# Contrast adjustment of 48 image planes: twelve 4 MB tiles in six buffers become six 8 MB tiles in three

## The chip, the cores and the metric

The kernel runs on one core of one Trainium2 chip. The metric is device time in microseconds (us) of one execution; the time of the kernel before is the median of three runs. The engines named below are TensorE (PE, matrix multiply), VectorE (DVE), ScalarE (ACT), GpSimd (POOL) and SyncE (SP). SP issues the loads and ACT issues the stores; both kinds of transfer run on the core's 16 DMA engines, loads through the queue that the profile calls q1 and stores through q10. On-chip memory has 128 partitions.

## The reference

The input is 16 images of 3 colour planes of 512 x 512 float32, so 48 planes of 262,144 pixels, 50.33 MB. Each plane is stretched around its own mean and clipped to 0..1:

```python
mean = np.mean(x, axis=(2, 3), keepdims=True)
return np.clip(mean + factor * (x - mean), 0, 1)     # factor = 1.5
```

That is `factor * x + (1 - factor) * mean`, so a plane must have been read in full before its first pixel can be written. Input and output together are 100.66 MB of traffic.

## The kernel before, in words

The input is seen as one flat array. `ROW = 8192` consecutive pixels (32 KB) lie in one partition, so a tile of 128 partitions holds 4 MB, which is four whole planes of 32 partitions each. There are twelve tiles and a `ring` of six buffers; tile `t` lives in buffer `t % 6` and is worked on in place. For each tile:

- `load` (L74, issued by SP) brings it in. At the start the kernel issues tile 0, tile 1, tiles 2 and 3 as one transfer and tiles 4 and 5 as one.
- `add` (L89, ACT) goes over the tile with a copy that also sums each partition's row.
- `shift_by` (L94, PE) multiplies the column of 128 row sums with `blockw`, a 128 x 128 matrix that holds `(1 - factor) / pixels` in blocks of 32 x 32 on its diagonal and zero elsewhere. So each partition gets the bias of its plane, in `bias` in PSUM. `blockw` is filled by POOL at the start (L59 and L61).
- `clip` is two VectorE instructions over the tile: times factor plus bias (L78), then max with 0 and min with 1 (L82).
- `store` (L99, issued by ACT) writes it out.

Tile 0 is treated apart: VectorE sums its first 4352 columns (L108) while ACT sums the other 3840, and it is clipped and stored in three column pieces of 1024, 2048 and 5120 pixels (`CUTS`). The other tiles go through in one piece.

The order is written out by hand (`manual_schedule`): each engine runs its instructions in program order, and waits are put in where data or a buffer is needed. In ACT's program, `add(t + 1)` comes before `store(t)`, so a store is issued after the next tile has landed. In SP's program, the load of tile `t + 6` waits until the store of tile `t`, which used the same buffer, has landed.

Of the kernel before, what the change touches and what calls it, by code (L numbers as in the profile page):

```python
# [1 line left out]

# [4 lines left out]


P = 128  # L10
ROW = 8192
BUFS = 6
CUTS = (0, 1024, 3072, ROW)
SUM = 4352


@with_exitstack
def kernel(
    ctx: ExitStack,
    tc: tile.TileContext,  # L20
    x: bass.AP,
    factor: float,
    out: bass.AP,
):

    nc = tc.nc
    f32 = mybir.dt.float32
    Alu = mybir.AluOpType  # L30
    Act = mybir.ActivationFunctionType

    B, C, H, W = x.shape
    n_img, n_pix = B * C, H * W
    ppi = n_pix // ROW
    per_tile = P // ppi
    n_tiles = n_img // per_tile
    assert ppi * ROW == n_pix and per_tile * n_tiles == n_img

    factor = float(factor)  # L40
    wconst = (1.0 - factor) / float(n_pix)

    x_f = x.rearrange("b c h w -> (b c h w)")
    out_f = out.rearrange("b c h w -> (b c h w)")

    def dram(ap, t, c0=0, c1=ROW):
        return bass.AP(tensor=ap.tensor, offset=t * P * ROW + c0, ap=[[ROW, P], [1, c1 - c0]])

    consts = ctx.enter_context(tc.tile_pool(name="consts", bufs=1))
    xpool = ctx.enter_context(tc.tile_pool(name="xpool", bufs=1))  # L50
    small = ctx.enter_context(tc.tile_pool(name="small", bufs=1))
    psum = ctx.enter_context(tc.tile_pool(name="psum", bufs=1, space=bass.MemoryType.PSUM))


    sums = small.tile([P, 2 * n_tiles], f32, name="sums")
    bias = psum.tile([P, n_tiles], f32, name="bias")

    blockw = consts.tile([P, P], f32, name="blockw")
    nc.gpsimd.memset(blockw, 0.0)  # L59
    for a in range(0, P, ppi):  # L60
        nc.gpsimd.memset(blockw[a : a + ppi, a : a + ppi], wconst)  # L61


    ring = xpool.tile([P, BUFS, ROW], f32, name="ring")

    def load(t, c0=0, c1=ROW, n=1):

        b = t % BUFS
        src = bass.AP(
            tensor=x_f.tensor,  # L70
            offset=t * P * ROW + c0,
            ap=[[ROW, P], [P * ROW, n], [1, c1 - c0]],
        )
        nc.sync.dma_start(out=ring[:, b : b + n, c0:c1], in_=src)  # L74

    def clip(t, c0, c1):
        part = ring[:, t % BUFS, c0:c1]
        nc.vector.tensor_scalar(  # L78
            out=part, in0=part, scalar1=factor, scalar2=bias[:, t : t + 1],
            op0=Alu.mult, op1=Alu.add,  # L80
        )
        nc.vector.tensor_scalar(  # L82
            out=part, in0=part, scalar1=0.0, scalar2=1.0, op0=Alu.max, op1=Alu.min
        )

    def add(t, c0=0):
        part = ring[:, t % BUFS, c0:ROW]
        own = sums[:, 2 * t : 2 * t + 1]
        nc.scalar.activation(out=part, in_=part, func=Act.Copy, accum_out=own)  # L89
        return own  # L90

    def shift_by(t, *parts):
        for k, part in enumerate(parts):
            nc.tensor.matmul(  # L94
                bias[:, t : t + 1], blockw, part, start=k == 0, stop=k == len(parts) - 1
            )

    def store(t, c0, c1):
        nc.scalar.dma_start(out=dram(out_f, t, c0, c1), in_=ring[:, t % BUFS, c0:c1])  # L99

    with tc.manual_schedule():
        load(0)
        load(1)
        load(2, n=2)
        load(4, n=2)

        rest = sums[:, 1:2]
        nc.vector.tensor_reduce(  # L108
            out=rest, in_=ring[:, 0, 0:SUM], axis=mybir.AxisListType.X, op=Alu.add
        )  # L110
        shift_by(0, add(0, SUM), rest)
        for c0, c1 in zip(CUTS[:-2], CUTS[1:-1]):
            clip(0, c0, c1)
            store(0, c0, c1)
        clip(0, CUTS[-2], ROW)
        own = add(1)
        store(0, CUTS[-2], ROW)
        load(BUFS)
        for t in range(1, n_tiles):
            shift_by(t, own)  # L120
            clip(t, 0, ROW)
            if t + 1 < n_tiles:
                own = add(t + 1)
            store(t, 0, ROW)
            if t + BUFS < n_tiles:
                load(t + BUFS)


# [1 line left out]
_INS = ['x', 'factor']  # L130
_OUTS = [((16, 3, 512, 512), 'float32')]

_NUMBERS = {'factor': 1.5}


# [26 lines left out]
```

## Time and profile before

| what | value |
|---|---|
| time, median of 3 runs | 239.19 us (239.05 to 239.28) |
| the profiled execution: its span, first to last instruction | 237.8 us |
| VectorE busy | 112.1 us (47%) |
| ScalarE busy | 82.9 us (35%) |
| TensorE busy | 7.6 us (3%) |
| traffic | 100.66 MB, mean 423 GB/s over the span |
| ACTIVATE over 128 x 8192 | 7.03 us |
| TENSOR_SCALAR over 128 x 8192, first and second | 4.49 and 4.43 us |
| store of 4096 KB, issue to landing (median) | 44.2 us |
| load of 4096 KB, issue to landing (median) | 33.3 us |

The span is the profiled execution's own time, counted on the core; what lies around it is not recorded for that execution. A row of the profile that is a group of instructions names the source line, the engine and the operation, what is written and read, the shapes and the count, then busy time and the mean of one in ns, then the idle time of the engine before them and what ended it. A row in the order of time starts with the start and the duration in us; what stands in brackets is how long the engine had been idle and who released it. "ACTq" and "SPq" are the sequencers of ACT and SP, which issue transfers. A row of a stretch gives the stretch, its length, the busy time of PE, of the weight loads, of DVE, ACT and POOL with instruction counts, then the TensorE clock, the mean busy share of the DMA engines, and GB/s. In the row that starts with DMA, each digit is the busy share of one fortieth of the span, in tenths.

The trace also holds a record of each DMA packet, with its queue, size, start and duration.

### The profile page before, as it was taken

Reading aid. Unit: us, or ns where it says so; the run is one execution under the profiler, and the core shown is the slowest. Engines: PE = TensorE matmul, PEld = TensorE weight load, DVE = VectorE, ACT = ScalarE, POOL = GpSimd, SP = SyncE. Lnnn points to the kernel's source line nnn. Section 1 sums busy time; section 2 is a strip of 40 time slices with the busy share of each in tenths; the row PEclk is TensorE's granted clock in tenths of the full one; section 3 lists DMA queues with packets and bytes.
Section 4 is the critical chain, followed back from the end, with each engine's and each line's share of the span. In section 5 each row is a group of like instructions: output and inputs, shape, how many; then the busy total and the mean of one; then the engine's idle time right before and its main releaser. Section 6 shows DMA issues by size and latency. Waiting matters only on the chain.

```text
span 237.8 us, 219 instructions
## 1 busy us (share of the span) xinstructions
PE 7.6 (3%) x26; PEld 6.5 (3%) x26; DVE 112.1 (47%) x29; ACT 82.9 (35%) x25; POOL 0.9 (0%) x9
## 2 busy tenths in 40 slices
PE   0010000000000000000000000000000000000000
PEld 0000000000000000000000000000000000000000
DVE  0078786009990039979407705902920950770000
ACT  2051900399000697380091083056038009100000
POOL 1000000000000000000000000000000000000000
DMA  7999999999999999999999999999999999999996
GB/s 265 441 441 442 401 471 429 391 413 430 457 441 435 413 408 430 435 435 441 441 441 441 441 435 435 402 419 430 435 441 441 441 441 441 441 430 413 413 430 259
DMA packets 3712, 100.66 MB, mean 423 GB/s; under 512 B 384, under 2 KB 384, under 8 KB 512
## 3 DMA queue, kind: packets, MB, share of 16 engines
q1 hardware_dynamic: 1696, 50.33, 49.6%
q10 hardware_dynamic: 2016, 50.33, 49.1%
HBM read 50.33 MB, written 50.33 MB: 423 GB/s over the span
## 4 chain that ended last, share of the span: by engine, by line
DMA 52%; another core or an unknown queue 15%; DVE 11%; issue 9%; PE 1%; ACT 1%; SPq 0%; ACTq 0%
DMA ring<-in_x_dram 33%; DMA out_dram<-ring 20%; DVE ring L78 6%; DVE ring L82 6%; PE bias L94 1%; ACT ring L89 1%; SPq L74 0%; ACTq L99 0%; ACTq L89 0%
## 5 line engine op out<-in xcount | busy, mean ns | idle before, releaser
L89 ACT ACTIVATE ring<-ring 128x8192 f32<-128x8192 f32 (+1 forms) x12 | 80.7, 6725 | 119.4 <-DMA ring<-in_x_dram 119.4
L78 DVE TENSOR_SCALAR ring<-ring,bias 128x8192 f32<-128x8192 f32 (+3 forms) x14 | 54.3, 3880 | 87.1 <-PE bias L94 87.1
L82 DVE TENSOR_SCALAR ring<-ring 128x8192 f32<-128x8192 f32 (+3 forms) x14 | 53.4, 3817 | 0.5
L94 PE MATMUL bias<-sums,blockw 128*128 128x1 f32 x26 | 7.6, 361 | 196.1 <-ACT ring L89 195.6
L94 PEld LDWEIGHTS bias<-sums,blockw 128*128 128x128 f32 x26 | 6.5, 311 | 197.1 <-ACT ring L89 179.9
L108 DVE TENSOR_REDUCE sums<-ring 128x1 f32<-128x4352 f32 x1 | 4.7, 4686 | 13.0 <-DMA ring<-in_x_dram 13.0
L89 ACT ACTIVATION_READ_ACCUMULATOR ring<-ring 128x1 f32 x12 | 2.2, 186 | 0.0
L89 ACT ACT_TABLE_LOAD x1 | 1.3, 1283 | 0.7 <-PEq L143 0.7
L61 POOL MEMSET blockw<- 32x32 f32 x4 | 0.5, 116 | 0.2
L59 POOL MEMSET blockw<- 128x128 f32 x1 | 0.2, 205 | 0.3 <-POOLq L143 0.3
L143 POOL MEMSET const-bfloat16-1.0<- 128x1 bf16 x1 | 0.1, 111 | 0.0
L143 POOL MEMSET const-uint8-127<- 128x1 uint8 x1 | 0.1, 111 | 0.0
L143 POOL MEMSET const-float32-1.0<- 128x1 f32 x1 | 0.1, 108 | 0.0
L143 POOL MEMSET const-float32-0.0<- 128x1 f32 x1 | 0.1, 103 | 0.2 <-issue 0.2
## 6 DMA issues: line engine op xcount, KB each, us to landing
out_dram<-ring ACTq DMA_DIRECT2D x11, 4096.0 KB, 44.2
ring<-in_x_dram SPq DMA_DIRECT2D x8, 4096.0 KB, 33.3
ring<-in_x_dram SPq DMA_DIRECT2D x2, 8192.0 KB, 60.6
out_dram<-ring ACTq DMA_DIRECT2D x1, 2560.0 KB, 37.5
out_dram<-ring ACTq DMA_DIRECT2D x1, 1024.0 KB, 25.9
out_dram<-ring ACTq DMA_DIRECT2D x1, 512.0 KB, 16.1
```

Of the source, the lines that this page charges most:

```text
L59: nc.gpsimd.memset(blockw, 0.0)
L61: nc.gpsimd.memset(blockw[a : a + ppi, a : a + ppi], wconst)
L78: nc.vector.tensor_scalar(out=part, in0=part, scalar1=factor, scalar2=bias[:, t : t + 1], op0=Alu.mult, op1=Alu.add,)
L82: nc.vector.tensor_scalar(out=part, in0=part, scalar1=0.0, scalar2=1.0, op0=Alu.max, op1=Alu.min)
L89: nc.scalar.activation(out=part, in_=part, func=Act.Copy, accum_out=own)
L94: nc.tensor.matmul(bias[:, t : t + 1], blockw, part, start=k == 0, stop=k == len(parts) - 1)
L108: nc.vector.tensor_reduce(out=rest, in_=ring[:, 0, 0:SUM], axis=mybir.AxisListType.X, op=Alu.add)
L143: nc = _bacc.Bacc("TRN2", target_bir_lowering=False, num_devices=1)
```

## The change

A row becomes 16384 pixels (64 KB), so a tile holds 8 MB, which is eight planes of 16 partitions each, and there are six tiles. The ring has three buffers of 64 KB per partition, as many bytes as before. Tile 0 is loaded in two column halves (a half is 32 KB per partition), and so is the last tile; the other loads are one transfer of the whole tile. ACT sums every tile in two halves, whose two sums are added by the matmul; the last tile's second half is shared between VectorE (4352 columns) and ACT (3840). The last tile is clipped and stored in two halves; every other tile is clipped in two instructions over 16384 columns and stored as a whole. `blockw` is filled with the constant, and two `affine_select` instructions zero what lies off the diagonal blocks, in place of four small memsets. In ACT's program, a store goes ahead of the next tile's first `add`, except for tiles 0, 1 and 4, where it comes after it.

```diff
-ROW = 8192
-BUFS = 6
-CUTS = (0, 1024, 3072, ROW)
+ROW = 16384
+HALF = ROW // 2
+BUFS = 3
 SUM = 4352
...
-    nc.gpsimd.memset(blockw, 0.0)
-    for a in range(0, P, ppi):
-        nc.gpsimd.memset(blockw[a : a + ppi, a : a + ppi], wconst)
+    nc.gpsimd.memset(blockw, wconst)
+    for base, sign in ((0, 1), (ppi - 1, -1)):
+        nc.gpsimd.affine_select(
+            out=blockw, in_=blockw, compare_op=Alu.is_ge, fill=0.0, base=base,
+            pattern=[[-sign * ppi, per_tile], [0, ppi]], channel_multiplier=sign,
+        )
...
+    def add(t, k, c0, c1):
+        part = ring[:, t % BUFS, c0:c1]
+        own = sums[:, 3 * t + k : 3 * t + k + 1]
+        nc.scalar.activation(out=part, in_=part, func=Act.Copy, accum_out=own)
+        return own
...
-        load(0)
-        load(1)
-        load(2, n=2)
-        load(4, n=2)
-
-        rest = sums[:, 1:2]
+    last = n_tiles - 1
+    with tc.manual_schedule():
+        load(0, 0, HALF)
+        load(0, HALF, ROW)
+        for t in range(1, BUFS):
+            load(t)
+        shift_by(0, add(0, 0, 0, HALF), add(0, 1, HALF, ROW))
+        clip(0)
+        for t in range(last):
+            late = t + 1 < BUFS or t + 1 == last
+            if not late:
+                store(t)
+            first = add(t + 1, 0, 0, HALF)
+            if late:
+                store(t)
+            if t + BUFS < last:
+                load(t + BUFS)
+            elif t + BUFS == last:
+                load(last, 0, HALF)
+                load(last, HALF, ROW)
+            if t + 1 < last:
+                shift_by(t + 1, first, add(t + 1, 1, HALF, ROW))
+                clip(t + 1)
+        rest = sums[:, 3 * last + 2 : 3 * last + 3]
         nc.vector.tensor_reduce(
-            out=rest, in_=ring[:, 0, 0:SUM], axis=mybir.AxisListType.X, op=Alu.add
+            out=rest, in_=ring[:, last % BUFS, HALF : HALF + SUM],
+            axis=mybir.AxisListType.X, op=Alu.add,
         )
-        shift_by(0, add(0, SUM), rest)
-        for c0, c1 in zip(CUTS[:-2], CUTS[1:-1]):
-            clip(0, c0, c1)
-            store(0, c0, c1)
-        clip(0, CUTS[-2], ROW)
-        own = add(1)
-        store(0, CUTS[-2], ROW)
-        load(BUFS)
-        for t in range(1, n_tiles):
-            shift_by(t, own)
-            clip(t, 0, ROW)
-            if t + 1 < n_tiles:
-                own = add(t + 1)
-            store(t, 0, ROW)
-            if t + BUFS < n_tiles:
-                load(t + BUFS)
+        shift_by(last, first, add(last, 1, HALF + SUM, ROW), rest)
+        for c0 in (0, HALF):
+            clip(last, c0, c0 + HALF)
+            store(last, c0, c0 + HALF)
```

More of the change, by code (lines that the diff above doesn't have):

```diff
@@ L37 @@
     n_tiles = n_img // per_tile
-    assert ppi * ROW == n_pix and per_tile * n_tiles == n_img
+    assert ppi * ROW == n_pix and per_tile * n_tiles == n_img and n_tiles > BUFS
     factor = float(factor)
@@ L44, with dram @@
     out_f = out.rearrange("b c h w -> (b c h w)")
-    def dram(ap, t, c0=0, c1=ROW):
+    def dram(ap, t, c0, c1):
         return bass.AP(tensor=ap.tensor, offset=t * P * ROW + c0, ap=[[ROW, P], [1, c1 - c0]])
@@ L52, with load, store, shift_by @@
     psum = ctx.enter_context(tc.tile_pool(name="psum", bufs=1, space=bass.MemoryType.PSUM))
-    sums = small.tile([P, 2 * n_tiles], f32, name="sums")
+    sums = small.tile([P, 3 * n_tiles], f32, name="sums")
     bias = psum.tile([P, n_tiles], f32, name="bias")
     blockw = consts.tile([P, P], f32, name="blockw")
-    nc.gpsimd.memset(blockw, 0.0)
-    for a in range(0, P, ppi):
-        nc.gpsimd.memset(blockw[a : a + ppi, a : a + ppi], wconst)
-    ring = xpool.tile([P, BUFS, ROW], f32, name="ring")
[L66 to L76, printed above, removed]
+    nc.gpsimd.memset(blockw, wconst)
[4 more added lines that the diff above has]
+        )
+    ring = xpool.tile([P, BUFS, ROW], f32, name="ring")
+    def load(t, c0=0, c1=ROW):
+        nc.sync.dma_start(out=ring[:, t % BUFS, c0:c1], in_=dram(x_f, t, c0, c1))
+    def store(t, c0=0, c1=ROW):
+        nc.scalar.dma_start(out=dram(out_f, t, c0, c1), in_=ring[:, t % BUFS, c0:c1])
+    def add(t, k, c0, c1):
[3 more added lines that the diff above has]
+        return own
+    def shift_by(t, *parts):
+        for k, part in enumerate(parts):
+            nc.tensor.matmul(
+                bias[:, t : t + 1], blockw, part, start=k == 0, stop=k == len(parts) - 1
+            )
+    def clip(t, c0=0, c1=ROW):
         part = ring[:, t % BUFS, c0:c1]
@@ L84, in clip @@
         )
[L86 to L99, printed above, removed]
```

## The prediction

> **What bounds the kernel now.** I read the DMA part of the profile first, because the kernel does almost no arithmetic per byte, then the stretches, then the order of time, where I looked for anything that waits while the DMA engines are idle.
>
> ```profile
> span 237.8 us, 219 instructions
> DMA  7999999999999999999999999999999999999996
> DMA packets 3712, 100.66 MB, mean 423 GB/s; under 512 B 384, under 2 KB 384, under 8 KB 512
> q1 hardware_dynamic: 1696, 50.33, 49.6%
> q10 hardware_dynamic: 2016, 50.33, 49.1%
> ```
>
> The 16 DMA engines are full from the second slice to the last but one; the two queues (q1 loads, q10 stores) take 98.7% of them. No compute engine comes near: VectorE (DVE) is at 47%.
>
> ```profile
> 62.00:198.00 136.00, 4.09 (x14) 3.50 (x14) 71.56 (x17) 51.80 (x15) 0.00 (x0) 1.00 1.00 431
> 198.00:237.00 39.00, 0.59 (x2) 0.50 (x2) 8.92 (x2) 5.07 (x2) 0.00 (x0) 1.00 0.96 416
> ```
>
> The DMA share is 1.00 for 136 us at 431 GB/s, and the last 39 us are stores alone. In the order of time:
>
> ```profile
> 13.01 3.40 ACT L89 ACTIVATE ring<-ring 128x3840 f32<-128x3840 f32 x1 [10.98 <-DMA ring<-in_x_dram]
> 13.01 4.69 DVE L108 TENSOR_REDUCE sums<-ring 128x1 f32<-128x4352 f32 x1 [13.01 <-DMA ring<-in_x_dram]
> 18.38 0.76 DVE L78 TENSOR_SCALAR ring<-ring,bias 128x1024 f32<-128x1024 f32 x1 [0.68 <-PE bias L94]
> 195.94 7.03 ACT L89 ACTIVATE ring<-ring 128x8192 f32<-128x8192 f32 x1 [12.26 <-DMA ring<-in_x_dram]
> 196.00 0.34 ACTq L99 DMA_DIRECT2D out_dram<-ring  x1
> 203.75 4.49 DVE L78 TENSOR_SCALAR ring<-ring,bias 128x8192 f32<-128x8192 f32 x1 [10.44 <-PE bias L94]
> 208.27 4.43 DVE L82 TENSOR_SCALAR ring<-ring 128x8192 f32<-128x8192 f32 x1
> 212.73 0.34 ACTq L99 DMA_DIRECT2D out_dram<-ring  x1
> ```
>
> The last store is issued at 212.73, yet the span ends at 237.8: 25 us of queued stores still run. Compute has slack; only DMA work, and moments with nothing in either queue, can move the end.
>
> The packet records (start, duration, size and queue of each) give the prices. One packet is one partition's row: 4 KB 0.159 us, 8 KB 0.309, 20 KB 0.761, 32 KB 1.213. Eight rows per engine make a 4 MB transfer. Stores alone start 9.68 us apart (196.77, 206.45, 216.13, 225.81); with both queues full the loads start 19.36 apart (116.90, 136.26, 155.62), so the queues alternate packet by packet with nothing lost. The account of before: first packet 1.76; the third 4 MB load starts at 21.72; 18 transfers until 196.77 take 175.05 = 18 x 9.68 + 0.81; three more 29.04; the last one with the engines' spread 10.83; then 1.17 to the end. Sum 237.81. The median of the runs is 239.19, so 1.37 lies outside the span; I add it unchanged.
>
> **The change, part by part.** Bytes are equal, so I sum the same account.
>
> Start: load 0's first half is again 4 MB in 32 KB rows, so 21.72 stands as the start of tile 1's load. The affine_selects take the place of four memsets (0.58 us on POOL). No row shows one: at best it saves that 0.58, at worst it costs what hides it. blockw is first needed when tile 0's sum is complete, at 22.74 + 7.03 + 0.19 = 29.96 in place of 16.62; POOL had finished at 1.6. 28 us hide it: 0.
>
> Counts: 12 ACTIVATEs, 26 matmul instructions and 15 VectorE instructions remain; two sweeps of clip over 16384 columns go by the slope (4.49 - 2.89)/3072 to 8.75, the second to 8.70, 17.5 us for a tile.
>
> The 0.81 goes: cutting the first store in 4, 8 and 20 KB rows costs 8 x (0.159 + 0.309 + 0.761 - 1.213) = 0.13, and 0.72 more is the excess of load packets over 1.213 between 33.5 and 62 us, where these small packets alternate with 32 KB ones. After that stretch the excess is 0.02.
>
> Packets of 64 KB are not in the trace. By the slope (1.213 - 0.159)/28 KB a packet has 0.0084 us fixed, so 64 KB takes 2.4176, and a tile 19.29 against 19.36: nine such transfers save 0.60. Upper end: no saving (19.36). I take the slope, since four sizes lie on it.
>
> Mixing returns once: load 5's 32 KB packets against store 3's 64 KB ones, eight pairs per engine. The 4 KB stretch (23.5 to 33.5) lost 0.01, the 20 KB one (47.4 to 62) 0.43 in 15 us, so 0 to 0.8 in 29 us; I take 0.4.
>
> Sum: 21.72 + 9 x 19.29 + 3 x 9.68 + 10.83 + 1.17 + 0.4 = 236.8, plus 1.37: 238.2, 1.0 below before.
>
> Does every queue stay full? Three things are worked out. (a) A landing is seen 0.4 us after its last packet when the other queue is empty (the last four stores: 0.39 to 0.43) and one packet of the other queue later when it is not (stores at 64.04 and 83.40 are seen 1.54 to 1.57 later); with 64 KB packets that is 0.4 + 2.4 = 2.8. (b) From issue to first packet an idle engine takes 1.0 (0.74 to 1.76); into busy engines it took 3.6 to 4.9 (19.89 to 23.49 and 24.76), 2.6 to 3.9 of it behind two or three 32 KB packets; this doubles if the wait counts packets, and stays if it counts bytes. (c) ACT's queue passes a late store once add's input has landed, not when add ends (store at 45.65 beside the ACTIVATE at 45.64).
> Tile 1 lands at 22.33 + 19.29 + 0.4 = 42.0. Tile 0's sum is complete at 29.96, matmul 0.6, clip until 48.1: store 0 issued. Load 2 and store 0 keep the engines full until 80.2. Store 1 needs clip 1: 42.0 + 14.4 + 0.7 + 17.5 = 74.6, and load 2, which ACT awaits first, at most 73: in the queue at 75.6, 4.6 us to spare. Load 3 waits on SP for store 0; its first packet is d after 80.2, d = 0.4 + issue to first packet = 4.0 to 5.3, or 6.6 to 9.3 if packets count. Store 1 runs alone meanwhile, so load 3 ends at 118.8 + d, and store 1 at 118.8 - d. Store 2 (ready at 102) then ends at 157.4 - d; load 5 can follow load 4 (ends 157.4) if it is queued by then: 157.4 - d + 2.8 + 1.05, so for every d above 3.9. Store 3: 118.8 + d + 2.8 + 14.4 + 0.7 + 17.5 = 154.2 + d; ACT stands in that wait, and add 4 is behind it, so store 4 comes another 32.6 later, at 186.8 + d, in the queue at 187.8 + d. Store 3 and load 5 keep the engines until 196.4. At d = 8 nothing is missing. Load 5b is seen by 199.2; reduce and matmul take 5.4 as at 13.01 to 18.38, a half clip 8.95: store 5a is in the queue at 214.6, store 4 ends at 215.7, 1.1 to spare.
>
> **The rivals.**
> 1. Store 4 late. If the wait for a busy engine counts packets in full, d = 9.3 and store 4 is queued at 197.1 while the engines ran dry at 196.0 (196.4 with the mixing): up to 1.1 us idle, 1:1 on the end, from d = 8.2 to 8.6 on. For it: add 4 stands behind store 3 on ACT. Against: it needs the upper end. 238.2 + 0.8 = 239.0, at most 239.3.
> 2. The change does not make 64 KB packets: the rows are cut in two. For it: no packet over 32 KB is seen. Against: every row so far was one packet. Then there is neither the 0.60 nor unequal packets: 21.72 + 174.24 + 29.04 + 10.83 + 1.17 + 1.37 = 238.4.
> 3. The other side: unequal packets cost more. The eight pairs of load 5 and store 3 replace the removed mixing with a longer one. Load packets in the worst moments (48.7 to 52) took 1.40 in the mean and up to 1.85, 0.19 to 0.64 over 1.213. Without mixing the time is 237.8; it becomes slower than before by 0.2% from an excess of 0.23 per pair. At 0.32, 2.6 us: 240.4; at 0.64, 242.9. Against: the mixing stretch as a whole averaged 0.05.
> 4. Rows 64 KB apart slow all packets. If every packet ran like the loads of 47.4 to 62 (1.268, 4.5% over), 232 us of them would become 242.5: 249. Against: 32 KB apart shows no trace of it, loads and stores alike at 1.213 from 62 us on.
> The Trainium skill (DMA: Bandwidth & Descriptors, Latency and other measured facts) has copies slow down where rows lie a large power of two apart, 207 GB/s per direction at 512 KiB against 214 with padding; by that figure, an estimate, 232 us would become 240, so 246. The trace of before, at 32 KB, does not show the effect, and the page has no row at 64 KB.
>
> **How the numbers follow.** A difference of about 0.2% (0.48 us: 238.7 to 239.7) is what a measurement of this kernel can tell. Main case 0.40 (238.2, own range 237.7 to 238.7: no mixing cost to 0.8, slope or a bit less); rows cut in two 0.15 (238.4); store 4 late 0.15 (238.7 to 239.3); unequal packets 0.15 (239.7 to 242.9); pitch 0.06; anything unseen 0.09, which I count as 0.02 no change and 0.07 slower. Faster: 0.40 + 0.13 of the cut rows + 0.01 = 0.54. Same: 0.02 + 0.14 of the late store + 0.02 = 0.18. Slower: the rest, 0.28. The range 237.6 to 240.6 leaves out the pitch, the upper third of the unequal packets, and parts of the unseen: about 0.19.
>
> **What would show it.** Right: largest packets of 64 KB at about 2.418; the second load half starting no later than 12.1; loads near 1.213 until 60 us; DMA share 1.00 in the middle; store 4 issued before 195.4; stores following without a break from 196 on, and the last store issued near 222 with the end at 236.8. Wrong: a slice in the DMA row below 9 around 80, 157, 196 or 215 (a queue ran dry, and the instruction issued right after names the wait), load packets of 166 to 196 well over 1.26 (rival 3), or all 64 KB packets over 2.43 (rival 4). The prediction falls outright if the engines idle for more than 1.5 us anywhere.

## The result, and the profile after

| | median, us | all runs, us |
|---|---|---|
| before | 239.12 | 238.68 to 239.28 (6 runs) |
| changed | 243.41 | 241.91 to 250.99 (6 runs) |

The changed kernel is slower: ratio 1.0155, 95% interval 1.0132 to 1.0178, about 3.7 us, where 238.2 and a gain of 0.4% had been forecast. The ratio leaves out executions more than 1.5% above the fastest of their kernel, but four of the twelve executions that the changed kernel had in all (246.6 to 251.0 us) are of that kind and are told here, since the mechanism found below makes such times. The wide spread is part of the result: the kernel before varies by 0.6 us.

Some words for what follows. Load 5a and 5b are the two halves of the last tile's load, store 5a and 5b its two stores. A row is the one packet that carries a partition's row; the completion packet is the packet of 4 bytes that each engine writes behind its rows of a transfer. A landing is seen when the instruction that waits for it starts. The excess of a packet is what it took beyond the straight line through the packet sizes of the kernel before; a stall is a moment at which many packets have an excess at once. Idle time and excess are means of the 16 engines, and the tail is the stretch from 197 us on. The records do not name a packet's engine; packets are put on one engine here where one ends as the next starts.

The profiled execution took 241.91 us, with a span of 240.2 (before: 237.8). Its page, first the summary and the DMA rows (busy tenths and GB/s in 40 slices of 6.0 us, packets, queues):

```profile
span 240.2 us, 183 instructions
DMA  7999989899898989898989899998998998988995
GB/s 273 426 437 437 524 349 524 349 349 524 349 524 349 524 349 513 360 513 360 513 360 502 360 480 393 458 415 355 442 508 360 431 518 355 524 349 355 415 404 235
DMA packets 2160, 100.66 MB, mean 419 GB/s; under 512 B 240, under 2 KB 240, under 8 KB 240
q1 hardware_dynamic: 1152, 50.33, 49.3%
q10 hardware_dynamic: 1008, 50.33, 48.6%
```

There are fewer packets (2160 for 3712): the 64 KB rows really are single packets, 512 on the load queue and 640 on the store queue, with a median of 2.418 us in both. The GB/s row swings between 349 and 524 because it counts each long packet whole, in one slice; the DMA digits change between 8 and 9 for the same reason. Stretches of the same execution (columns as before, the last two DMA share and GB/s):

```profile
62.00:200.00 138.00, 4.10 (x14) 3.51 (x14) 64.46 (x8) 49.52 (x14) 0.00 (x0) 1.00 1.00 431
200.00:240.00 40.00, 1.17 (x4) 1.00 (x4) 22.43 (x5) 3.50 (x2) 0.00 (x0) 1.00 0.88 380
216.00:218.40 2.40, 0.00 (x0) 0.00 (x0) 2.40 (x2) 0.00 (x0) 0.00 (x0) 1.00 0.48 205
```

The middle is as full as before, where a packet that takes too long counts as busy too. The last 40 us are emptier, 0.88 for 0.96, and around 217 the engines are half idle. In the order of time:

```profile
190.90 7.03 ACT L75 ACTIVATE ring<-ring 128x8192 f32<-128x8192 f32 x1 [13.51 <-DMA ring<-in_x_dram]
195.63 0.34 ACTq L70 DMA_DIRECT2D out_dram<-ring  x1
203.05 3.40 ACT L75 ACTIVATE ring<-ring 128x3840 f32<-128x3840 f32 x1 [5.02 <-DMA ring<-in_x_dram]
203.05 4.69 DVE L121 TENSOR_REDUCE sums<-ring 128x1 f32<-128x4352 f32 x1 [7.50 <-DMA ring<-in_x_dram]
217.46 9.24 ACTq L70 DMA_DIRECT2D out_dram<-ring  x2
```

190.90 is load 5a being seen, 195.63 the issue of store 4, 203.05 load 5b being seen, 217.46 the issue of store 5a. On 15 of the 16 engines store 4 had drained by 217.2, and store 5a's first packet starts at 218.30.

By the packet records, the 2.35 us of span between the two profiled executions are made of: idle engines between first and last packet, 2.51 for 1.12 us in the mean of 16 (1.33 of it from 215 to 219); excess of packets, 2.69 for 1.33 us (1.29 of it at 50.7 to 51.1, where all 16 load packets took 3.4 to 3.9 us, and 0.39 at 158.4 to 158.7, in store packets); less 0.7 for fewer packets and the missing small ones. Sum 2.0; 0.3 is not assigned.

### The profile page after: what moved, and what is told of

The parts are those of the page before. It is cut to its first block, busy times and chain, and to the rows that moved or that the text cites. A ratio compares the mean times of both kernels' runs of the same rounds, so it can differ in the third digit from the quotient of the medians.

```text
span 240.2 us, 183 instructions
## 1 busy us (share of the span) xinstructions
PE 7.6 (3%) x26; PEld 6.5 (3%) x26; DVE 109.7 (46%) x15; ACT 82.7 (34%) x25; POOL 1.1 (0%) x7
## 2 busy tenths in 40 slices
DMA packets 2160, 100.66 MB, mean 419 GB/s; under 512 B 240, under 2 KB 240, under 8 KB 240
## 4 chain that ended last, share of the span: by engine, by line
DMA 53%; another core or an unknown queue 23%; DVE 9%; ACT 6%; SPq 1%; issue 1%; PE 0%; ACTq 0%; DVEq 0%
DMA ring<-in_x_dram 35%; DMA out_dram<-ring 18%; ACT ring L75 6%; DVE ring L86 4%; DVE ring L90 4%; DVE sums L121 2%; SPq L67 1%; PE bias L80 0%; ACTq L70 0%; DVEq L86 0%
## 5 line engine op out<-in xcount | busy, mean ns | idle before, releaser
L86 DVE TENSOR_SCALAR ring<-ring,bias 128x16384 f32<-128x16384 f32 (+1 forms) x7 | 52.8, 7538 | 108.9 <-PE bias L80 108.9
L90 DVE TENSOR_SCALAR ring<-ring 128x16384 f32<-128x16384 f32 (+1 forms) x7 | 52.3, 7475 | 0.2
L80 PE MATMUL bias<-sums,blockw 128*128 128x1 f32 x26 | 7.6, 361 | 200.8 <-ACT ring L75 200.2
L80 PEld LDWEIGHTS bias<-sums,blockw 128*128 128x128 f32 x26 | 6.5, 311 | 201.8 <-ACT ring L75 181.1
L59 POOL TENSOR_SCALAR_AFFINE_SELECT blockw<-blockw 128x128 f32<-128x128 f32 x2 | 0.7, 342 | 0.1
```

Source lines behind the costliest of these rows:

```text
L59: nc.gpsimd.affine_select(out=blockw, in_=blockw, compare_op=Alu.is_ge, fill=0.0, base=base, pattern=[[-sign * ppi, per_tile], [0, ppi]], ...
L80: nc.tensor.matmul(bias[:, t : t + 1], blockw, part, start=k == 0, stop=k == len(parts) - 1)
L86: nc.vector.tensor_scalar(out=part, in0=part, scalar1=factor, scalar2=bias[:, t : t + 1], op0=Alu.mult, op1=Alu.add,)
L90: nc.vector.tensor_scalar(out=part, in0=part, scalar1=0.0, scalar2=1.0, op0=Alu.max, op1=Alu.min)
```

## The experiments

Two theories. A: the tail. Load 5b lands late, so store 5a is issued after store 4 has drained. B: long packets stall, whatever the tail does. Medians and ranges are over all executions of the kernel; the median of the kernel before is 238.98 to 239.05 beside each.

**The changed kernel again.**

> The changed kernel once more, for the spread of its time and a second look at where its DMA engines idle or stall. Theory A (late last store): the first half of tile 5 is stored too late, because load 5b is seen only at 203 us; the profile shows an idle of 1.3 us or more of the 16 engines just before that store, and a slower execution has a longer one. Theory B (long packets): the 64 KB packets themselves stall (at 50.7 us all 16 took 3.4 to 3.9 us in place of 2.418, at 158.4 2.6 to 3.1); a slower execution has more or longer stalls and the idle stays at 1.3. Both: time 242 to 244 us.

244.1 us, 240.66 to 249.1; the profiled one is the execution of 249.1. Its page, then its stretches and the order of time:

```profile
span 247.4 us, 183 instructions
DMA  7999797999998989999898989899899998903996
```

```profile
217.00:226.40 9.40, 0.00 (x0) 0.00 (x0) 9.37 (x3) 0.00 (x0) 0.00 (x0) 1.00 0.07 28
```

```profile
160.52 7.03 ACT L75 ACTIVATE ring<-ring 128x8192 f32<-128x8192 f32 x1 [21.28 <-DMA ring<-in_x_dram]
192.89 0.34 ACTq L70 DMA_DIRECT2D out_dram<-ring  x1
211.22 4.69 DVE L121 TENSOR_REDUCE sums<-ring 128x1 f32<-128x4352 f32 x1 [18.41 <-DMA ring<-in_x_dram]
225.63 9.25 ACTq L70 DMA_DIRECT2D out_dram<-ring  x2
```

From 217 to 226.4 hardly a packet starts (DMA share 0.07), and by the packet records the engines idle 8.0 us between store 4 and store 5a. Of the 7.2 us between this execution and the first, idle makes 6.0 and stalls 1.2: A, mainly. The surprise is the direction. Here store 4 was issued 2.7 us *earlier* (192.89 for 195.63), and load 5b was seen 8.2 us *later* (211.22 for 203.05). The packet records show why: store 4's 64 KB rows came in while the engines still had rows of load 5b, and a load row of 1.21 us then waits for a store row of 2.42. From store 4's first row on (196.94), 22 of load 5b's 128 rows were still to start. Most engines are done with load 5b by 201.2, but its last four rows end at 205.8, 205.9, 207.8 and 208.4, and the landing counts the slowest. In the first execution store 4's first row came at 197.40, and only two rows of load 5b started later, both on one engine: 15 engines were done by 197.9, that one at 200.25, and its completion packet stood behind a row of store 4 until 202.67. What made store 4 early is one row: load 4's last row ended at 160.14 here, its completion packet (4 bytes) followed at once, and the landing was seen at 160.52; in the first execution the last row ended at 160.46, a row of store 3 got in (160.45 to 162.87), the completion packet came at 162.87, and the landing was seen at 163.26.

**The last tile stored in quarters.**

```diff
-        for c0 in (0, HALF):
-            clip(last, c0, c0 + HALF)
-            store(last, c0, c0 + HALF)
+        for c0 in range(0, ROW, HALF // 2):
+            clip(last, c0, c0 + HALF // 2)
+            store(last, c0, c0 + HALF // 2)
```

> The last tile is clipped and stored in four quarters in place of two halves, so its first store is issued after 4.5 us of clipping in place of 8.9. Theory A: the idle before it goes, 1.3 to 1.6 us less than the changed kernel, span near 238.7, and the runs lie closer together. Theory B: the stalls stay, at most 0.3 us less on the stalls' side, so the time stays near 242.5; an idle of 1.3 us that goes without the end moving would also speak for B.

242.67 us (242.36 to 242.96, 4 executions). The idle before store 5 is gone (15 to 16 engines busy throughout 216 to 219, though load 5b was seen only at 205.9) and no execution is long; but the profiled span is 240.8. Its engines now lose 2.5 us at the very end: most finish by 237.0, the last one at 239.5. That last one is also the engine that ended load 5b last, at 203.1: having fallen behind, it stays behind. Cutting the last chain removes the long idle and not the unevenness: A can explain the spread, not the median. That no execution is long could be luck here: where a third of them are, as with the changed kernel, four in a row without one come about once in five times.

**32 KB packets.** 64 bytes are put between the two halves of a row in the buffer, so a whole-tile transfer consists of 32 KB packets; tiles, waits and order are the same.

```diff
+PAD = 16
...
-    ring = xpool.tile([P, BUFS, ROW], f32, name="ring")
+    ring = xpool.tile([P, BUFS, 2, HALF + PAD], f32, name="ring")
...
+    def whole(ap, t):
+        return bass.AP(tensor=ap.tensor, offset=t * P * ROW, ap=[[ROW, P], [HALF, 2], [1, HALF]])
```

> The changed kernel with its rows laid in the buffer as two halves with 64 bytes between, so that a whole-tile transfer consists of 32 KB packets while everything else (tiles, buffers, waits, order) stays. Theory B: the stalls of 1.7 us in all go, span near 238.5 to 239, and the spread of the runs falls to that of the kernel before (0.6 us). Theory A: load 5 and store 3 then share the engines one to one in place of one to two, load 5b lands some 4 us earlier, and the idle at the tail goes; span 238.5 to 239 as well, but by the tail: the profile tells which. If the time stays at 242 or more, the packet size has nothing to do with it. 72 more packets per engine cost at most 0.6 us.

240.85 us (239.27 to 241.95), 1.0068 of before (1.0042 to 1.0095). The DMA rows of its page and its order of time:

```profile
DMA  7999999999999999999999999999999999999995
GB/s 263 439 439 439 439 439 439 439 346 439 439 428 433 433 422 417 417 439 439 439 439 439 439 433 439 439 422 395 417 439 433 439 428 433 433 433 439 433 433 219
```

```profile
191.86 0.54 ACTq L83 DMA_DIRECT2D out_dram<-ring  x1
198.15 4.69 DVE L134 TENSOR_REDUCE sums<-ring 128x1 f32<-128x4352 f32 x1 [6.36 <-DMA ring<-in_x_dram]
212.56 9.25 ACTq L83 DMA_DIRECT2D out_dram<-ring  x2
```

Store 4 was issued even earlier, at 191.86, and load 5b was seen at 198.15: no idle in the tail. The records show the order reversed: load 5 was issued at 156.0, before load 4 ended (159.2), and store 3 (issued 157.5) came in behind it at 162.1 and shared one to one until 198.5. Store 4 stood behind store 3. In the changed kernel store 2 landed later, so load 5 was issued only at 158.48, after store 3 had the engines (158.35); with rows twice as long store 3 took two thirds, drained at 187.8, and left its queue open for store 4. One dip remains in the GB/s row, 346 in the ninth slice (47.8 to 53.7). It holds the stall of all 16 load packets at 49.5 to 50.0, just ahead of the first store's first packet (53.17); from 48 to 52 us the load packets lose 1.1 us. The edit does a little more than cut packets: it also moves the second half of each row on the chip by 64 bytes, and no run has that alone.

**Store 4 after load 5b.** One store is moved on ACT's queue.

```diff
-            if late:
+            if late and t + 1 < last:
                 store(t)
...
+        own = add(last, 1, HALF + SUM, ROW)
+        store(last - 1)
-        shift_by(last, first, add(last, 1, HALF + SUM, ROW), rest)
+        shift_by(last, first, own, rest)
```

> The changed kernel with one store moved on ACT's queue: store 4 is issued after load 5b has landed (after ACT's last add), not after load 5a. Theory A (a race at 197 us): every row of load 5b that an engine still has when store 4 joins waits behind a 64 KB store packet, 1.2 + 2.4 = 3.6 us a row, and the landing waits for the slowest engine; that is what makes store 5a late and the time anything from 240.7 to 251. Then load 5b lands near 198.5 in every execution, store 4 starts some 1.5 to 2 us later on idle engines, there is no idle before store 5a, the time is 240.5 to 242 and its spread is below 1.5 us, with no run over 243.5. Rival B (the stalls of packets make the spread): the time moves by less than 0.7 from 243 to 244 and runs near 247 or above still appear.

243.6 us (242.17 to 244.04, 5 executions): no long one, as A said (by chance five in a row come about once in eight times), but the median is above the range that was expected. The stretch around the store and the order of time:

```profile
197.00:202.00 5.00, 0.58 (x2) 0.50 (x2) 1.12 (x1) 2.46 (x3) 0.00 (x0) 1.00 0.57 242
```

```profile
200.88 4.69 DVE L121 TENSOR_REDUCE sums<-ring 128x1 f32<-128x4352 f32 x1 [5.57 <-DMA ring<-in_x_dram]
200.96 0.34 ACTq L70 DMA_DIRECT2D out_dram<-ring  x1
215.29 9.24 ACTq L70 DMA_DIRECT2D out_dram<-ring  x2
```

The idle before store 5a is gone and has become an idle before store 4, 3.7 us in place of the 1.5 to 2 expected: 14 engines end load 5b by 198.3, two of them at 200.2 and 200.51, and all wait for the slowest. So the tail costs either way, at a different place.

**Less work before store 4.** The second clip sweep of tile 4 (max and min) is left out, so that tile's pixels are not clipped.

```diff
-    def clip(t, c0=0, c1=ROW):
+    def clip(t, c0=0, c1=ROW, both=True):
...
+        if both:
...
-                clip(t + 1)
+                clip(t + 1, both=t + 1 != last - 1)
```

> The changed kernel without the second clip sweep of tile 4 (the max and min are left out for that tile alone, so its pixels are not clipped). Store 4 can then be issued when load 5a has landed, near 190.9 us, in place of 195.6. Theory A (the race): less work makes the kernel slower. Store 4 joins near 193 to 194, when each engine still has three or four rows of load 5b; each of them now waits for a 64 KB store packet of 2.42 us, so load 5b ends at 205 to 207.5 in place of 200, is seen 2.8 later, and store 5a is in the queue 15.2 after that, at 223 to 225.5, while store 4 has drained near 217.7: 5.5 to 8 us of idle engines in place of 1.3, time 246 to 249 in nearly every execution. Rival (an earlier store keeps the engines fuller, and the stalls set the time): 243 or less.

251.33 us, 251.05 to 251.55: 7 to 8 us *slower* than the changed kernel's medians with less work, in every execution; ratio to before 1.0514. The order of time and the idle stretch:

```profile
191.28 0.34 ACTq L70 DMA_DIRECT2D out_dram<-ring  x1
213.57 4.69 DVE L122 TENSOR_REDUCE sums<-ring 128x1 f32<-128x4352 f32 x1 [28.65 <-DMA ring<-in_x_dram]
227.98 9.24 ACTq L70 DMA_DIRECT2D out_dram<-ring  x2
```

```profile
217.00:228.80 11.80, 1.17 (x4) 1.00 (x4) 11.03 (x4) 0.06 (x1) 0.00 (x0) 1.00 0.01 6
```

A's direction is shown; its size was low (246 to 249 expected). Load 5b ended at 210.8, not 205 to 207.5: store 4 came in at 195.0 to 196.8, later than assumed, and yet the slowest engine still had four rows of load 5b to go, each behind a store row.

**The same edit with 32 KB packets.**

> The kernel with rows cut in 32 KB packets, without the second clip sweep of tile 4 (its max and min are left out). With 64 KB rows this edit cost 8 us. Theory A says why it did: store 3 had drained at 189, so an earlier store 4 went in against load 5b. With 32 KB rows store 3 is still in the store queue until 198, because load 5 was queued first and the two share one to one; an earlier store 4 then only stands behind store 3. So no change: 240.2 to 241.5, load 5b seen near 198. Rival (any earlier store delays load 5b): 244 or more.

240.08 us (239.64 to 241.69): no harm.

```profile
182.96 0.54 ACTq L83 DMA_DIRECT2D out_dram<-ring  x1
197.65 4.69 DVE L135 TENSOR_REDUCE sums<-ring 128x1 f32<-128x4352 f32 x1 [14.73 <-DMA ring<-in_x_dram]
```

Store 4's first row came at 197.32, behind store 3, when load 5b had ended (196.05). So the early store did harm where the store queue in front of it was empty, and none where it was not. The two kernels differ in packet size too, so this pair alone does not separate the two. The profiled executions side by side; "rows of 5b behind" are the rows of load 5b that start after store 4's first row on any engine:

| execution | store 4 issued | its first row | rows of 5b behind | load 5b seen | idle in the tail | its time |
|---|---|---|---|---|---|---|
| less work before store 4 | 191.3 | 195.0 | 43 | 213.6 | 10.5 | 251.4 |
| changed, second look | 192.9 | 196.9 | 22 | 211.2 | 8.0 | 249.1 |
| small first pieces (below) | 194.8 | 197.1 | 4 | 205.8 | 4.1 | 243.8 |
| changed, first look | 195.6 | 197.4 | 2 | 203.1 | 1.3 | 241.9 |
| store 4 after load 5b | 201.0 | 201.8 | 0 | 200.9 | 3.7, before store 4 | 243.8 |
| 32 KB packets | 191.9 | 197.5 | 0 | 198.1 | 0 | 240.7 |
| 32 KB packets, less work | 183.0 | 197.3 | 0 | 197.7 | 0 | 240.2 |

**32 KB packets and quarters at the end.** The edits of 32 KB packets and of the last tile in quarters, together.

> The kernel with rows cut in 32 KB packets (240.85), and with the last tile stored in quarters as well. If what it still loses against the kernel before (1.8 us) is a late store 5a in its slower executions, the quarters take it away: 239.3 to 239.8, spread under 1 us. If it is the stalls of packets in the middle (1.1 us near 50 and 0.55 near 160 in its profile), it stays at 240.3 to 241.2.

240.81 us (239.72 to 241.65), as with 32 KB packets alone: what these still lose is not a late store 5.

**The first store: small pieces taken out of the kernel before.**

```diff
-        for c0, c1 in zip(CUTS[:-2], CUTS[1:-1]):
-            clip(0, c0, c1)
-            store(0, c0, c1)
-        clip(0, CUTS[-2], ROW)
+        clip(0, 0, ROW)
         own = add(1)
-        store(0, CUTS[-2], ROW)
+        store(0, 0, ROW)
```

> The kernel before with one edit: tile 0 is clipped and stored whole, not in pieces of 1024, 2048 and 5120 columns. The sum of the prediction has 0.81 us for these small packets: by it the time falls from 239.1 to 238.3. If small store packets cost nothing in the end (the engines are as full, only in another order), the time stays at 239.1; if the later first store costs something, it rises.

240.15 us (239.25 to 240.49), slower by 0.44% (interval 0.30 to 0.58), 1.1 us where the sum had a gain of 0.81. The GB/s row of its page:

```profile
GB/s 264 440 440 440 440 352 440 440 440 435 440 440 440 424 429 413 424 429 440 435 440 440 440 440 440 429 429 424 407 429 435 440 440 440 440 440 440 440 418 204
```

A like dip, 352 in the sixth slice (29.8 to 35.7), stands where the first store comes in (first packet 32.21). In this profiled execution (239.97 us, span 238.2 for 237.8) the excess sums to hardly more than in the kernel before (1.41 and 1.33), so the stall does not account for the 1.1 us.

**Tile 0 of the kernel before in two halves** (`CUTS = (0, 4096, ROW)`, 16 KB packets).

> The kernel before with tile 0 cut in two halves of 4096 columns (16 KB packets), not in 1024, 2048 and 5120; its first store is issued near 23 us, in place of 19.9, and 27.3 with tile 0 whole. If the loss with tile 0 whole (1.17 us) comes from its late start, most of it goes: 239.0 to 239.4. If it comes from the missing small packets, it stays: 239.8 to 240.2.

238.88 us (238.73 to 239.55), ratio 0.9995 (0.9986 to 1.0004): no difference from before. With the previous run: pieces in 16 KB packets issued from 23 us on are as good as pieces in packets of 4, 8 and 20 KB from 20 on; the whole tile in 32 KB packets at 27.5 is not. Whether the time of issue or the packet size does it, these two runs do not separate.

**Small first pieces put into the changed kernel**, 1024, 2048 and 13312 columns.

```diff
-        clip(0)
+        for c0, c1 in ((0, 1024), (1024, 3072)):
+            clip(0, c0, c1)
+            store(0, c0, c1)
+        clip(0, 3072, ROW)
...
-                store(t)
+                store(t, 3072 if t == 0 else 0, ROW)
```

> The changed kernel with tile 0 clipped and stored in pieces of 1024, 2048 and 13312 columns, as the kernel before cut its tile 0. Theory S1 (small first packets let the store queue join softly): the stall of 1.1 to 1.3 us that all 16 engines show about 3 us after the first store is issued shrinks to 0.5 or less, and the time falls by 0.6 to 1. Theory S2 (the stall belongs to the joining, whatever its packets): it is as long in sum, only earlier, near 34 to 48 us, and the time stays within 0.5 of 243 to 244.

243.82 us (243.15 to 244.67). Load packets between 30 and 65 us lose 0.9 us for 1.3, but the time does not follow: this execution idles 4.1 us before store 5a. The tail covers the answer. So the same edit was tried where the tail has no idle:

**Small first pieces with 32 KB packets**, 1024, 2048, 5120 and 8192 columns.

> The kernel with rows cut in 32 KB packets, and tile 0 stored in pieces of 1024, 2048, 5120 and 8192 columns. If its remaining loss of 1.8 us against the kernel before is the stall where the first store joins the full load queue (1.1 us near 50 in its profile, 0.7 in all in the kernel before), the early small pieces take it down: 239.6 to 240.2. If not, 240.4 to 241.3, as with 64 KB rows, where this edit changed nothing.

239.66 us (239.36 to 240.43), 1.0028 of before (1.0019 to 1.0038); 1.2 us less than with 32 KB packets alone, and less than half the spread. The GB/s row of its page:

```profile
GB/s 265 441 441 441 436 441 403 406 433 440 410 468 425 425 408 425 441 441 441 436 441 441 441 430 419 408 425 441 441 441 436 441 441 441 430 419 408 425 441 265
```

The dip to 346 is gone; load packets lose 0.5 us between 35 and 65, not 1.1.

**Every tile in halves**, each half with its own load, waits and store.

```diff
+        def halves(do, t):
+            for c0 in (0, HALF):
+                do(t, c0, c0 + HALF)
...
-            load(t)
+            halves(load, t)
...
-        clip(0)
+        halves(clip, 0)
...
-                store(t)
+                halves(store, t)
```

> The changed kernel with every tile loaded, clipped and stored in two column halves, each with its own transfer and its own waits: 32 KB packets as in the kernel with rows cut in two (240.85), but a load follows half a store and a store half a clip. Theory G (an 8 MB unit lets the two queues run empty and refill late): load 5b is done before 195, no idle at the tail, 239.0 to 239.5. Theory P (only the size of the packets matters): as with the cut rows, 240.3 to 241.4.

242.99 us (242.45 to 243.29): neither theory. There is no idle before store 5a, but the excess is 3.08 us, the most of the kernels with 32 KB packets, much of it in small stalls where the store queue changes from one transfer to the next (82, 102, 121, 141, 161, 181 us), and the engines end unevenly, between 236.8 and 239.5. Finer waits do not mend the change; why this kernel stalls more is open.

## Why the prediction was wrong

**What held.** 64 KB rows are one packet of 2.418 us (forecast 2.4176), so the rival of cut rows falls; with that median on both queues the rival of rows 64 KB apart falls too. The Trainium skill (DMA: Bandwidth & Descriptors, Latency and other measured facts) tells of slower copies at large power-of-two pitches; at 64 KB no run here shows it. The affine_selects took 0.68 us under cover. The early timeline came out: tile 1 seen at 41.84 (42.0), store 0 issued at 47.87 (48.1), store 1 at 74.23 (74.6). Load 5's packets against store 3's cost next to nothing (an excess of 0.07 us from 166 to 196 in the first execution), so neither the 0.4 for mixing nor rival 3 was needed.

**How far the sum was off.** The sum gave a span of 236.8; the profiled execution, one of the shortest, took 240.2. Engines idle 1.4 us more than in the kernel before, and of the 2.69 us of excess the sum holds 0.6 (at the start, as before) and 0.4 (the mixing), so 1.7 more; 0.3 is not assigned. The longer executions add to this in the tail.

**The step that failed first: "The 0.81 goes".** I read the excess of load packets between 33.5 and 62 us as the price of the small pieces. Without them the kernel before lost as much (0.69 us between 12 and 65 us, for 0.72) and took 1.1 us more; with them the kernel of 32 KB packets gained 1.2. The sum had the sign wrong, about 2 us in all. What stands in that stretch of the changed kernel is a stall about 3 us after its first store is issued, for which the sum has no term. Between 12 and 65 us the load packets of the profiled executions lost 0.5 to 0.9 us where the first store goes in small pieces or in packets of 16 KB, 0.7 to 1.3 where it starts with packets of 32 KB, and 1.1 to 1.5 with 64 KB. That the store queue's entry makes the stall is read from its place, 3 to 4 us ahead of the first store packet. In the kernel before it does not hold: its first store packet came at 23.49, its excess at 34, at 40 and from 46 to 52 us, and the cause of that is not shown.

**The step that failed most: "Store 3 and load 5 keep the engines until 196.4 ... Load 5b is seen by 199.2".** It was seen at 203.05 in one execution and at 211.22 in the other. Four parts of it, with the order of time of the first execution:

```profile
155.73 0.34 ACTq L70 DMA_DIRECT2D out_dram<-ring  x1
158.48 0.96 SPq L67 DMA_DIRECT2D ring<-in_x_dram  x2
163.26 7.03 ACT L75 ACTIVATE ring<-ring 128x8192 f32<-128x8192 f32 x1 [25.78 <-DMA ring<-in_x_dram]
```

First, the order of load 5 (issued at 158.48) and store 3 (at 155.73) was the reverse of the forecast. Store 2 was to start right behind store 1, between 109.5 and 114.8; its first packet came at 119.66. The packet records show why: on each engine store 1's last row (on the first engine until 114.78) is followed by a load row, then store 1's completion packet alone (117.19), then another load row, and only then store 2. The completion packet takes a turn of its own; I had counted that for landings and not for the next transfer. With d = 5.6 as measured (load 3's first packet came at 85.81, the forecast has it d after 80.2), store 2 was to end at 151.8 and load 5 to be issued at 154.6; store 2's last row ended at 155.61. Load 3 had the engines alone while store 2 was awaited, and ended at 120.55 instead of 124.4, so store 3 was ready at 155.73 instead of 159.8. Store 4 then hung on load 4, seen at 163.26, and not on ACT's wait for store 3.

Second, with store 3 in front at two thirds, load 5b was left for last and store 3 left its queue empty at 187.8.

Third, for d = 5.6 I had store 4 in the queue at 193.4 and let it stand idle beside load 5b until 196.4, while my own rule (the queues alternate packet by packet) sends it in between load 5b's rows. In the execution of 249.1 us it did so.

Fourth, the sum takes the engines as even, and a landing waits for the slowest. In the first execution 15 engines ended load 5b at 197.4 to 197.9 and one at 200.25. The 1.1 us to spare before store 5a was therefore not there, even where store 4 was late.

**Rival 1 had the place and not the sign.** It priced store 4 coming late. Store 4 coming *early* is the expensive side, 7 to 8 us more when issued 4.3 us earlier. The mark set in the prediction, "store 4 issued before 195.4" as right, is met by the two executions with the longest tails (191.28 and 192.89), and by the kernel with 32 KB packets (191.86), where it did no harm: it tells nothing by itself.

**What is settled.** Store 4 entering among load 5b's rows delays the end: issued earlier, it made every execution long, and the one long execution of the changed kernel that was profiled has it too; issued after load 5b, or with 32 KB packets behind a store queue that was still full, no execution was long. Of the 4.3 to 5.1 us between the medians of before and of the changed kernel, the edit to 32 KB packets takes away 2.6 to 3.3, the small pieces of the first store 1.2 more, and 0.65 remain with 8 MB tiles. These shares are differences of medians of kernels that spread by 1 to 2.7 us among themselves, and 32 KB packets are not enough by themselves: with tiles in halves, which have them too, the time is 242.99. Open are the rest of 0.65, the stalls with tiles in halves, what makes single engines fall behind, and the 1.1 us of the kernel before with its first store whole, of which its profile shows only part. No kernel tried beats the one before by more than can be measured; its variant with tile 0 in halves equals it.

## What to carry to other kernels

When two DMA queues share the engines, ask of a transfer that the end waits for what else can enter beside it: look at which queue runs empty shortly before the last load lands, and apply the sharing by packet size to whatever comes next in that queue. Here an earlier issue on the other queue cost more (7 to 8 us) than the work that it saved. Keeping the store out until the load had landed was no cure either, since the engines then idled. In a kernel whose engines are full, sum up the slowest engine and not only the mean: a landing waits for it. And measure a term before taking it out of the sum: here the small first pieces looked like a cost and were a gain.

## What the runs showed of the hardware

- A landing is seen 0.4 us after its last row when the completion packet follows at once (160.14 to 160.52), and 2.8 us after it when a 64 KB row of the other queue gets in between (160.46 to 163.26). Of the two executions that show this, the one with the earlier landing ended 7 us later.
- The completion packet takes a turn of its own: with 64 KB rows in both queues, the next store's first row came 4.9 us after the last row of the store before it on the same engine (114.78 to 119.66), two load rows later.
- Shortly before a store's first packet comes in beside a full load queue, all 16 load packets in flight lengthen at once: to 3.4 to 3.9 us for 2.418 with 64 KB packets (50.7 to 51.1), to at most 2.88 for 1.213 with 32 KB. With 16 KB pieces the excess was 0.4 us for two pieces, at the first 4 KB piece of the kernel before 0.01.
- From issue to first packet into busy engines it took 3.8 us with 64 KB rows in one place (82.04 to 85.81) and 6.5 in another, with the stall in it (47.87 to 54.41), against 3.6 for the first store of the kernel before.
